# High and low parts of x side by side: one 512-column product in place of two of 256

## The chip, the cores and the metric

One core of one Trainium2 chip. The metric is the device time of one execution in microseconds, median of three runs. Engines: PE multiplies matrices, DVE works on vectors, ACT does activations, copies and casts, POOL is GpSimd, and SP's queue issues most of the DMAs. Granted clock 1.00 is PE at 2.4 GHz, 0.5 is 1.2 GHz.

## What is computed

A decoder trunk for 256 tokens and 2048 channels in float32, with one even and one odd layer (the reference, cut):

```
h = rmsnorm(x, e_norm); z = h @ e_w_in            # 2048 x 6784
a_in, a_gate, q, kB, vB, b_gate = split(z)
yA = rwkv7_mix(a_in, ...)                         # token shift, recurrence over tokens, 16 heads x 64
yB = swa_sinks(rope(q), rope(kB), vB, sinks)      # window 128, 16 query heads, 4 key heads
x = x + concat(yA * silu(a_gate), yB * silu(b_gate)) @ e_w_out
h = rmsnorm(x, o_norm); u, vv, gate = split(h @ o_w_in)      # 2048 x 6144
x = x + (chunked_sgu(u, vv, ...) * silu(gate)) @ o_w_out
return rmsnorm(x, final_norm)
```

## The kernel before

Channels lie on partitions, and x is kept transposed as 16 blocks `k` of 128 channels x 256 tokens. All four weights stream from HBM once, in chunks of 128 x 1024 float32 (512 KB); there are 266 chunks.

**Products in parts.** PE multiplies float32r operands, which round a float32. So each operand is split into a high part (rounded to float32r) and a low part (what the rounding leaves), and a product is high x high + high x low + low x high. `chunk` (L265) loads `raw`, casts it on ACT to `wh`, and on DVE subtracts to get `wl`. These two are traced with priority, so that they stand ahead of other work in ACT's and DVE's queues, and each of the three buffers (`raw`, `wh`, `wl`) exists three times.

**Two kinds of tiles.** A tile of kind B (105 of them: 41 in the even input product, 32 in the odd one, 16 in each output product) gives 128 output channels for 256 tokens. A block of the weight is stationary and x streams: `half_b` (L275) issues three matmuls of 256 columns for each k, 8 k to a chunk, 2 chunks to a tile. The stationary operand is loaded for each matmul, also where two in a row have the same one. A tile of kind A (3 in the even layer for key/value and queries, 4 in the odd one) gives 512 output channels for 2 x 128 tokens: x is stationary, 512 weight columns stream, and `eighth_a` (L301) issues 12 matmuls of 512 columns for a chunk of 2 k. The results of both lie in a PSUM pool of three buffers of 512 columns, of which a B tile uses half.

**Order of the work.** `products` (L312) goes through the tiles. `done(i, ps)` takes a finished tile, and after each chunk `pace` (L257) lets a planner (`Later`, L142) trace further steps of the queued tasks (recurrence, attention, norms) between the chunks, as long as its estimate of DVE's and ACT's time is not ahead of its estimate of PE's. Those estimates come from `Timed`: for PE the columns / 2400 + 0.004 us for a float32r matmul (L135), for DVE elements / 960 + 0.06, for ACT elements / 1200 + 0.1. Engines then work in the order laid down when the program is built.

**What takes a finished tile** (PSUM to SBUF):
- Even layer, `e_done` (L1061): the first B tile carries the low-rank inputs (`scaled`, then `lora_task`, whose tanh lies before the low-rank products `pw`, `pa`); then 8 head pairs with three tiles each (keys, receptance, values), which `shift` (L595) reads from PSUM with one ACT and one DVE pass. Tiles before number X_NEW = 7 go through `scaled` (L589), one DVE pass that multiplies by the norm `rs1`. Then `k_task`, `r_task`, `v_task`: the keys end in `stk` (L688), which the products `m` (L715) need. 16 tiles are gates (`gate`, L1041): ACT's tanh and a DVE pass, both from PSUM. During the first eight gates the triangular solve (`solve_task`, L752) runs on DVE; during the queries and the last eight the recurrence and attention.
- Output product of the even layer, two passes over half of the rows each: `first_done` (L1113) adds a tile to x by one DVE pass, `resid_done` (L1125) adds it, splits the result for the next product (`x1h`, `x1l`) and squares it on POOL.
- Odd layer, `o_done` (L1201): the 32 B tiles are u (one DVE pass, times the norm) and gate, in turn, with `sgu_task` (L1188) behind every second one.
- Last product, `last_done` (L1228): one addition, then squares and scale; then the last norm.

**Around the start.** POOL computes rotary tables (`rope_tables`, L534) in small buffers with the tags of `k1` (L228), and, in between, masks (`setup_task`, L474), among them `blk`, `blkr` and `cen`. `msum` in `rms_rows` (L423) needs the buffer of tag "y", which the rotary table holds up to L570; `tt` of the rotary table holds tag "Pi" up to the end of the second `poly` (L557).

Of the kernel before, what the change touches and what calls it, by code (L numbers as in the profile page):

```python
# [109 lines left out]
class Hold(float):  # L110
    """for how many chunks a queue rests after a step"""


class Timed:
    """An engine with an estimate of how long its work takes, in us."""
# [26 lines left out]
class Later:  # L142
    """Work that is traced in between the chunks of the weight products, as far as the engines keep up."""
# [50 lines left out]
def kernel(ctx, tc, xT, w_in, w_out, o_in, o_out, cols, rows, loras, sinks, pos, ws_t, ws_b, out, dbg=None):  # L194
# [33 lines left out]
    def k1(s, tag, dt=F32):  # L228
        return t1.tile([P, 260], dt, tag=tag, bufs=2 if tag in ("kp", "rp", "vp") else 1, name=nm(s))
# [45 lines left out]
    def half_b(pss, drams, ah, al, half, first, last):  # L275
        for ps, d in zip(pss, drams):
            wh, wl = chunk(d)
            for k in range(8):
                kt = half * 8 + k
                c = slice(k * P, (k + 1) * P)  # L280
                for i, (w, a) in enumerate(((wh, ah), (wh, al), (wl, ah))):
                    TE.matmul(ps[:, 0:T], w[:, c], a(kt), start=(first and k == 0 and i == 0),
                              stop=(last and k == 7 and i == 2))

    def first_chunk(dram):
        """the first of all: in two halves, so that the products start early"""
# [7 lines left out]
        for i in range(2):  # L294
            c = slice(512 * i, 512 * i + 512)
            xh_of(i)
# [4 lines left out]
    def eighth_a(ps, dram, ah, al, q):  # L301
        wh, wl = first_chunk(dram) if not seen else chunk(dram)
        for k in range(2):
            kt = 2 * q + k
            c = slice(k * 512, (k + 1) * 512)
            for h in range(2):
                t = slice(h * P, (h + 1) * P)
                for i, (w, a) in enumerate(((wh, ah), (wh, al), (wl, ah))):
                    TE.matmul(ps[h], a(kt)[:, t], w[:, c], start=(kt == 0 and i == 0),
                              stop=(kt == NK - 1 and i == 2))  # L310

    def products(order, dram, ah, al, done, lead=0, halves=(0, 1)):  # L312
        """One pass over a weight (or over half of its rows); done(i, psum) takes each finished tile.
        The first `lead` tiles go by halves, so that the inputs of the second half may come late."""
# [5 lines left out]
        def tiles(ids):  # L320
            pss = [acc("ps") for _ in ids]
            for n, half in enumerate(halves):
                end = n == len(halves) - 1
                half_b(pss, [dram[base[i] + half] for i in ids], ah, al, half, n == 0, end)
# [7 lines left out]
        for i in range(lead, len(order)):  # L332
            if order[i][0] == "B":
                tiles([i])
            else:
                ps = (acc("psa"), acc("psb"))
                for q in range(8):
                    eighth_a(ps, dram[base[i] + q], ah, al, q)
# [24 lines left out]
    xh, xl = pairs_of(NK, "xh", F32R), pairs_of(NK, "xl", F32R)  # L363
# [5 lines left out]
    def xh_of(k):  # L369
        if state.get("normed"):  # L370
            return xn[k][0]
        if k not in seen:
# [3 lines left out]
            split(xh[k], xl[k], xs[:, k], col(C_GE, k))  # L376
        return xh[k]

    def xl_of(k):
        return xn[k][1] if state.get("normed") else xl[k]  # L380
# [4 lines left out]
    def scale_task():  # L385
        """x times its norm, split anew"""
        for q in range(8):
# [3 lines left out]
            h, l = pairs_of(2, "xnh", F32R), pairs_of(2, "xnl", F32R)  # L391
            for i in range(2):
                xn[2 * q + i] = h[i], l[i]
                split(h[i], l[i], xs[:, 2 * q + i], col(C_GE, 2 * q + i))
# [3 lines left out]
    # the tensor engine's clock is up when the first weights are in  # L398
# [12 lines left out]
    def newton(y, a):  # L411
        """y <- y (1.5 - 0.5 a y^2)"""
# [10 lines left out]
    def rms_rows(parts, rs):  # L423
        """rs[p, t] = (mean of squares over channels + eps)^-1/2 on every partition"""
# [9 lines left out]
    def rms_cols(parts, rc, mc):  # L434
        """the same with tokens on partitions: [P, 2], a column for each half"""
# [36 lines left out]
    sm = {}  # L472

    def setup_task():  # L474
# [6 lines left out]
        # decay weights over what their rounding leaves, and the other way round for the rates  # L481
# [6 lines left out]
        blk = const.tile([P, P], F32, name="blk")  # L488
# [41 lines left out]
    # rotary angles: position * inv_freq reduced by 2 pi, then sine and cosine of a quarter of it  # L530
# [51 lines left out]
    # ================= even layer =================  # L582
# [64 lines left out]
    def k_task(p, kp, st):  # L647
# [11 lines left out]
        # exp of the summed log decays, and of their negative  # L659
# [15 lines left out]
        # minus twice the normed key: the correction of y^-1/2 is (3 - ss y^2) / 2  # L675
# [5 lines left out]
        # minus the scaled keys here, their products with the written ones in the other half: they share  # L681
        # the products with the state and the values
# [69 lines left out]
    def solve_task():  # L752
        """(I - M)^-1 of every head and chunk: 32 x 32 blocks on VectorE, then the corner"""
# [551 lines left out]
```

## Time and profile before

| | |
|---|---|
| median of three runs | 920.48 us (919.36 to 920.57) |
| span of the profiled execution | 916.3 us |
| time of the profiled execution itself | not given beside the span; the median of the runs is 4.2 us above it |
| PE busy | 885.4 us, 7086 matmuls |
| DVE busy | 640.1 us |
| ACT busy | 498.5 us |
| POOL busy | 133.5 us |
| read from HBM | 148.45 MB, mean 164 GB/s |

A busy time is the union of an engine's instructions in the profiled execution. Matmuls are pipelined and the end of each is modelled, so their starts tell more than their durations. PEld are the loads of stationary operands, which overlap with PE. "idle before" is the time for which an engine stood before an instruction, with what ended it. Most instructions carry the line of one helper (L126), so groups are told apart by tiles, written out<-in.

### The profile page before, as it was taken

Reading aid. Unit: us, or ns where it says so; the run is one execution under the profiler, and the core shown is the slowest. Engines: PE = TensorE matmul, PEld = TensorE weight load, DVE = VectorE, ACT = ScalarE, POOL = GpSimd, SP = SyncE. Lnnn points to the kernel's source line nnn. Section 1 sums busy time; section 2 is a strip of 40 time slices with the busy share of each in tenths; the row PEclk is TensorE's granted clock in tenths of the full one; section 3 lists DMA queues with packets and bytes.
Section 4 is the critical chain, followed back from the end, with each engine's and each line's share of the span. In section 5 each row is a group of like instructions: output and inputs, shape, how many; then the busy total and the mean of one; then the engine's idle time right before and its main releaser. Section 6 shows DMA issues by size and latency. Waiting matters only on the chain.

```text
span 916.3 us, 17587 instructions
## 1 busy us (share of the span) xinstructions
PE 885.4 (97%) x7086; PEld 823.3 (90%) x7086; DVE 640.1 (70%) x1004; ACT 498.5 (54%) x823; POOL 133.5 (15%) x215
## 2 busy tenths in 40 slices
PE   7889999999999899999999999999999999999994
PEld 6759899999998677889999988889999999999994
DVE  6766888887899954577767965459766666665554
ACT  7557776676644585777544444447344344344441
POOL 8821100000000201000004840000000000004331
PEclk9968999999999999899999999999999999999997
DMA  8522555545555332234675787665555565565652
GB/s 277 166 89 69 164 162 161 168 154 161 156 148 185 135 93 71 70 100 143 195 224 180 264 262 213 193 193 182 176 178 176 175 182 177 171 182 183 185 164 92
DMA packets 44146, 151.68 MB, mean 166 GB/s; under 512 B 5153, under 2 KB 5537, under 8 KB 43809
## 3 DMA queue, kind: packets, MB, share of 16 engines
q1 hardware_dynamic: 43344, 149.52, 53.0%
q8 instruction: 55, 0.90, 0.4%
q10 hardware_dynamic: 720, 1.05, 0.3%
q14 instruction: 27, 0.21, 0.1%
HBM read 148.45 MB, written 2.10 MB: 164 GB/s over the span
## 4 chain that ended last, share of the span: by engine, by line
PE 81%; DVE 10%; POOL 4%; ACT 2%; issue 2%; DMA 1%; DVEq 0%; ACTq 0%; POOLq 0%
PE ps L126 61%; PE psa L126 6%; PE psb L126 5%; DVE wl L126 4%; PE py L126 2%; DVE dd L126 2%; DVE tmp L126 1%; PE pm L126 1%; ACT sc L126 1%; PE m L126 1%; PE po L126 1%; PE ptp L126 1%; PE pw L126 1%; ACT wh L126 1%; PE pa L126 1%
## 5 line engine op out<-in xcount | busy, mean ns | idle before, releaser
L126 DVE TENSOR_TENSOR wl<-raw,wh 128x1024 fp32r<-128x1024 f32 (+1 forms) x267 | 330.5, 1239 | 169.1 <-ACT wh L126 168.6
L126 ACT CAST wh<-raw 128x1024 fp32r<-128x1024 f32 (+1 forms) x267 | 278.6, 1044 | 310.6 <-PE ps L126 173.1
L126 PE MATMUL ps<-xnh,wh 128*128 128x256 f32 x560 | 161.6, 289 | 0.0
L126 PE MATMUL ps<-xnh,wl 128*128 128x256 f32 x560 | 159.8, 285 | 0.6 <-DVE wl L126 0.6
L126 PE MATMUL ps<-xnl,wh 128*128 128x256 f32 x560 | 159.1, 284 | 0.0
L126 PE MATMUL ps<-x1h,wh 128*128 128x256 f32 x512 | 146.1, 285 | 0.0
L126 PE MATMUL ps<-x1h,wl 128*128 128x256 f32 x512 | 144.9, 283 | 0.0
L126 PE MATMUL ps<-x1l,wh 128*128 128x256 f32 x512 | 144.8, 283 | 0.0
L126 PEld LDWEIGHTS ps<-xnh,wh 128*128 128x128 f32 x560 | 107.1, 191 | 2.0 <-issue 1.0
L126 PEld LDWEIGHTS ps<-xnh,wl 128*128 128x128 f32 x560 | 107.3, 192 | 1.4 <-DVE wl L126 0.8
L126 PEld LDWEIGHTS ps<-xnl,wh 128*128 128x128 f32 x560 | 107.2, 191 | 0.2 <-issue 0.2
L126 PEld LDWEIGHTS ps<-x1l,wh 128*128 128x128 f32 x512 | 98.2, 192 | 0.0
L126 PEld LDWEIGHTS ps<-x1h,wh 128*128 128x128 f32 x512 | 98.2, 192 | 0.0
L126 PEld LDWEIGHTS ps<-x1h,wl 128*128 128x128 f32 x512 | 98.2, 192 | 0.0
L126 PE MATMUL ps<-yk,wh 128*128 128x256 f32 x512 | 92.8, 284 | 0.0
L126 PE MATMUL ps<-yo,wh 128*128 128x256 f32 x512 | 92.3, 283 | 0.0
L126 PEld LDWEIGHTS ps<-yk,wh 128*128 128x128 f32 x512 | 79.8, 192 | 1.1 <-DVE x L126 0.8
L126 PEld LDWEIGHTS ps<-yo,wh 128*128 128x128 f32 x512 | 79.9, 192 | 0.0
L126 PE MATMUL ps<-yo,wl 128*128 128x256 f32 x256 | 72.4, 283 | 0.0
L126 PE MATMUL ps<-yk,wl 128*128 128x256 f32 x256 | 72.4, 283 | 0.0
L126 PEld LDWEIGHTS ps<-yo,wl 128*128 128x128 f32 x256 | 49.1, 192 | 0.0
L126 PEld LDWEIGHTS ps<-yk,wl 128*128 128x128 f32 x256 | 49.1, 192 | 0.0
(327 smaller groups left out, 1503.3 us busy)
## 6 DMA issues: line engine op xcount, KB each, us to landing
raw<-in_w_in SPq DMA_DIRECT2D x105, 512.0 KB, 3.7
raw<-in_o_in SPq DMA_DIRECT2D x96, 512.0 KB, 3.7
raw<-in_w_out SPq DMA_DIRECT2D x32, 512.0 KB, 3.7
raw<-in_o_out SPq DMA_DIRECT2D x32, 512.0 KB, 3.6
x<-in_xT SPq DMA_DIRECT2D x8, 256.0 KB, 4.1
xs<-in_xT SPq DMA_DIRECT2D x7, 256.0 KB, 6.5
wst<-in_ws_t SPq DMA_DIRECT2D x1, 1024.0 KB, 5.8
bsb<-in_ws_b SPq DMA_DIRECT2D x1, 1024.0 KB, 7.8
```

The costliest lines, as they stand in the source:

```text
L126: return f(*args, **kw)
```

## The change

x is no longer kept as one tile of high parts and one of low parts, but as one tile for each k with both, `[128, 2, 256]`. In `half_b` the high weights meet both parts in one matmul of 512 columns, whose result fills the whole PSUM buffer (high x high on the left, high x low on the right); the low weights meet the high part of x in a second matmul of 256 columns, added on the left. So a B tile leaves PSUM as two halves, which have to be added: `whole` copies the right half on ACT and adds the left half on DVE; the output products add both halves to x, one DVE pass each. Kind A keeps its three matmuls and only addresses x in another way.

To make room, small buffers have 256 in place of 260 columns (but for one), `blk` uses the small buffer with the tag "Pi" and is later read as `blkr`, and the tag "z" gets two buffers. Comments are removed.

```diff
     def k1(s, tag, dt=F32):
-        return t1.tile([P, 260], dt, tag=tag, bufs=2 if tag in ("kp", "rp", "vp") else 1, name=nm(s))
+        return t1.tile([P, 260 if tag == "Pp" else T], dt, tag=tag, bufs=2 if tag in ("kp", "rp", "vp", "z") else 1, name=nm(s))
...
-    def half_b(pss, drams, ah, al, half, first, last):
+    def half_b(pss, drams, xp, half, first, last):
         for ps, d in zip(pss, drams):
             wh, wl = chunk(d)
             for k in range(8):
-                kt = half * 8 + k
+                x = xp(half * 8 + k)
                 c = slice(k * P, (k + 1) * P)
-                for i, (w, a) in enumerate(((wh, ah), (wh, al), (wl, ah))):
-                    TE.matmul(ps[:, 0:T], w[:, c], a(kt), start=(first and k == 0 and i == 0),
-                              stop=(last and k == 7 and i == 2))
+                TE.matmul(ps.rearrange("p (s t) -> p s t", s=2), wh[:, c], x, start=(first and k == 0), stop=False)
+                TE.matmul(ps[:, 0:T], wl[:, c], x[:, 0], start=False, stop=(last and k == 7))
...
-                for i, (w, a) in enumerate(((wh, ah), (wh, al), (wl, ah))):
-                    TE.matmul(ps[h], a(kt)[:, t], w[:, c], start=(kt == 0 and i == 0),
+                for i, (w, s) in enumerate(((wh, 0), (wh, 1), (wl, 0))):
+                    TE.matmul(ps[h], xp(kt)[:, s, t], w[:, c], start=(kt == 0 and i == 0),
                               stop=(kt == NK - 1 and i == 2))
...
-    xh, xl = pairs_of(NK, "xh", F32R), pairs_of(NK, "xl", F32R)
+    def parts_of(n, s):
+        return [k2(s, F32R).rearrange("p (s t) -> p s t", s=2) for _ in range(n)]
+
+    xp = parts_of(NK, "xp")
...
-            h, l = pairs_of(2, "xnh", F32R), pairs_of(2, "xnl", F32R)
-            for i in range(2):
-                xn[2 * q + i] = h[i], l[i]
-                split(h[i], l[i], xs[:, 2 * q + i], col(C_GE, 2 * q + i))
+            for k, x in zip((2 * q, 2 * q + 1), parts_of(2, "xn")):
+                xn[k] = x
+                split(x[:, 0], x[:, 1], xs[:, k], col(C_GE, k))
                 yield
...
-        blk = const.tile([P, P], F32, name="blk")
+        blk = k1("blk", "Pi")[:, 0:P]
         G.memset(blk, 0.0)
         G.memset(blk[0:64, 0:64], 1.0)
         G.memset(blk[64:128, 64:128], 1.0)
         blkr = const.tile([P, P], F32R, name="blkr")
         G.tensor_copy(blkr, blk)
+        blk = blkr.bitcast(F32)
         cen = const.tile([P, P], F32, name="cen")
...
-    def scaled(ps):
-        z = k1("z", "z")[:, 0:T]
-        V.tensor_tensor(z, ps[:, 0:T], rs1, op=ALU.mult)
+    def whole(ps, z):
+        S.copy(z, ps[:, T:2 * T])
+        V.tensor_tensor(z, z, ps[:, 0:T], op=ALU.add)
         return z
 
+    def scaled(z):
+        V.tensor_tensor(z, z, rs1, op=ALU.mult)
+        return z
...
     def gate(ps, rs, dst, final=False):
         th = k1("th", "kp")[:, 0:T]
-        z = ps[:, 0:T]
+        z = whole(ps, dst)
         if rs is not None:
-            V.tensor_tensor(dst, z, rs, op=ALU.mult)
-            z = dst
+            V.tensor_tensor(z, z, rs, op=ALU.mult)
...
-            later.add("r", lora_task(scaled(ps)))
+            later.add("r", lora_task(scaled(whole(ps, k1("z", "z")[:, 0:T]))))
...
-            z = shift(ps if i >= X_NEW else scaled(ps), E_ORDER[i][1] // P, ("kp", "rp", "vp")[w])
+            z = whole(ps, k1("z", "z")[:, 0:T])
+            z = shift(z if i >= X_NEW else scaled(z), E_ORDER[i][1] // P, ("kp", "rp", "vp")[w])
...
     def first_done(i, ps):
-        V.tensor_tensor(x1[i], x1[i], ps[:, 0:T], op=ALU.add)
+        for s in range(2):
+            V.tensor_tensor(x1[i], x1[i], ps[:, s * T:(s + 1) * T], op=ALU.add)
...
     def resid_done(i, ps):
-        V.tensor_tensor(x1[i], x1[i], ps[:, 0:T], op=ALU.add)
-        split(x1h[i], x1l[i], x1[i], col(C_GO, i))
+        for s in range(2):
+            V.tensor_tensor(x1[i], x1[i], ps[:, s * T:(s + 1) * T], op=ALU.add)
+        split(x1p[i][:, 0], x1p[i][:, 1], x1[i], col(C_GO, i))
...
-            V.tensor_tensor(u, ps[:, 0:T], rs2, op=ALU.mult)
+            V.tensor_tensor(u, whole(ps, u), rs2, op=ALU.mult)
...
     def last_done(i, ps):
-        V.tensor_tensor(x1[i], ps[:, 0:T], x1[i], op=ALU.add)
+        for s in range(2):
+            V.tensor_tensor(x1[i], ps[:, s * T:(s + 1) * T], x1[i], op=ALU.add)
```

## Rows read from the trace of the kernel before

**Rows 1.** The page's parts 1 and 4: busy time of engines, chain that ended last.

```profile
PE 885.4 (97%) x7086; PEld 823.3 (90%) x7086; DVE 640.1 (70%) x1004; ACT 498.5 (54%) x823; POOL 133.5 (15%) x215
...
PE 81%; DVE 10%; POOL 4%; ACT 2%; issue 2%; DMA 1%; DVEq 0%; ACTq 0%; POOLq 0%
```

**Rows 2.** Stretches, instructions on `ps` alone: us from:to, length, busy by engine (count).

```profile
95.68:240.00 144.32, 131.96 (x1065) 128.61 (x1065) 10.33 (x22) 9.62 (x21) 1.00 0.54 162
...
355.00:435.00 80.00, 51.33 (x384) 48.22 (x383) 2.90 (x7) 2.83 (x8) 0.96 0.35 102
435.00:531.00 96.00, 93.36 (x768) 92.42 (x768) 13.28 (x32) 0.17 (x1) 1.00 0.68 220
...
619.00:811.00 192.00, 188.28 (x1538) 185.57 (x1539) 13.53 (x32) 0.00 (x0) 1.00 0.58 177
811.00:903.20 92.20, 92.16 (x768) 91.95 (x767) 6.41 (x17) 0.00 (x0) 1.00 0.53 160
```

**Rows 3.** The chain that ended last, in order of time: start us, us, what.

```profile
198.81 1.09 PE m L126 x16
...
811.00 92.17 PE ps L126 x768
```

**Rows 4.** Stretches: length, busy PE, PEld, DVE, ACT, POOL (count), PEclk, DMA share, GB/s.

```profile
56.00:79.96 23.96, 23.96 (x82) 17.23 (x83) 10.29 (x20) 12.81 (x26) 0.00 (x0) 0.56 0.13 42
79.96:99.73 19.77, 17.85 (x152) 17.39 (x151) 18.45 (x37) 13.38 (x28) 6.06 (x12) 1.00 0.41 133
...
198.58:218.35 19.77, 19.77 (x173) 19.51 (x172) 16.11 (x32) 13.60 (x26) 0.67 (x2) 1.00 0.52 162
240.00:301.00 61.00, 58.56 (x398) 53.03 (x396) 58.54 (x106) 27.60 (x40) 1.47 (x4) 1.00 0.53 162
...
400.00:420.00 20.00, 20.00 (x168) 17.80 (x166) 19.85 (x53) 15.48 (x44) 0.00 (x0) 1.00 0.48 137
435.00:482.00 47.00, 47.00 (x387) 45.11 (x384) 31.14 (x49) 23.14 (x42) 0.00 (x0) 1.00 0.67 208
503.28:511.92 8.64, 8.64 (x75) 8.64 (x74) 7.83 (x9) 4.48 (x7) 6.83 (x7) 1.00 0.60 192
619.00:811.00 192.00, 192.00 (x1605) 191.89 (x1604) 132.22 (x202) 85.53 (x110) 0.00 (x0) 1.00 0.58 177
```

**Rows 5.** Timeline of PE, a tile of kind A: start us, us, engine, instruction.

```profile
532.04 0.39 PE L126 MATMUL psb<-wl,x1h 128*128 128x512 f32 x1
...
533.40 0.39 PE L126 MATMUL psb<-wl,x1h 128*128 128x512 f32 x1
```

**Rows 6.** Timeline of PE at the low granted clock; nine matmuls lie between.

```profile
74.49 0.41 PE L126 MATMUL ps<-xl,wh 128*128 128x256 f32 x1
...
76.63 0.41 PE L126 MATMUL ps<-xh,wl 128*128 128x256 f32 x1
```

**Rows 7.** Groups of instructions by shape, DVE and ACT: busy us, mean ns, idle before.

```profile
L126 DVE TENSOR_TENSOR x<-x,ps 128x256 f32<-128x256 f32 x32 | 13.3, 415 | 11.0 <-PE ps L126 10.5 <-DMA x<-in_xT 0.5
...
L126 DVE SCALAR_TENSOR_TENSOR zp<-ps,colt,zp 128x255 f32<-128x255 f32 x19 | 9.1, 478 | 0.2
...
L126 ACT COPY qT<-pt 128x256 f32<-128x256 f32 x8 | 2.6, 382 | 0.0
```

**Rows 8.** Timeline of DVE in a settled head pair.

```profile
195.42 0.41 DVE L126 SCALAR_TENSOR_TENSOR stk<-y,aPi 64x256 f32<-64x256 f32 x1
195.75 0.41 DVE L126 TENSOR_TENSOR stk<-zp,Pi 64x256 f32<-64x256 f32 x1
...
196.53 0.42 DVE L126 TENSOR_TENSOR stk<-zp,Pi 64x256 f32<-64x256 f32 x1
...
197.38 1.22 DVE L126 TENSOR_TENSOR wl<-raw,wh 128x1024 fp32r<-128x1024 f32 x1
```

**Rows 9.** Timeline of POOL near the start.

```profile
5.50 0.76 POOL L493 CAST blkr<-blk 128x128 fp32r<-128x128 f32 x1
```

**Rows 10.** Timeline of DVE before the first norm, with the idle time before.

```profile
38.30 0.42 DVE L126 TENSOR_SCALAR msum<-rms 128x256 f32<-128x256 f32 x1 [3.08 <-POOL rt L570]
```

More of the change, by code (lines that the diff above doesn't have):

```diff
@@ L110 @@
 class Hold(float):
+    pass
 class Timed:
@@ L295, in first_chunk @@
             c = slice(512 * i, 512 * i + 512)
-            xh_of(i)
+            x_of(i)
             S.copy(wh[:, c], raw[:, c])
@@ L299, in first_chunk, with eighth_a @@
         return wh, wl
-    def eighth_a(ps, dram, ah, al, q):
+    def eighth_a(ps, dram, xp, q):
         wh, wl = first_chunk(dram) if not seen else chunk(dram)
@@ L307, in eighth_a, with products @@
                 t = slice(h * P, (h + 1) * P)
-                for i, (w, a) in enumerate(((wh, ah), (wh, al), (wl, ah))):
-                    TE.matmul(ps[h], a(kt)[:, t], w[:, c], start=(kt == 0 and i == 0),
+                for i, (w, s) in enumerate(((wh, 0), (wh, 1), (wl, 0))):
+                    TE.matmul(ps[h], xp(kt)[:, s, t], w[:, c], start=(kt == 0 and i == 0),
                               stop=(kt == NK - 1 and i == 2))
-    def products(order, dram, ah, al, done, lead=0, halves=(0, 1)):
+    def products(order, dram, xp, done, lead=0, halves=(0, 1)):
         base, at = [], 0
@@ L323, in tiles @@
                 end = n == len(halves) - 1
-                half_b(pss, [dram[base[i] + half] for i in ids], ah, al, half, n == 0, end)
+                half_b(pss, [dram[base[i] + half] for i in ids], xp, half, n == 0, end)
                 for i, ps in zip(ids, pss):
@@ L337, in products @@
                 for q in range(8):
-                    eighth_a(ps, dram[base[i] + q], ah, al, q)
+                    eighth_a(ps, dram[base[i] + q], xp, q)
                     if q == 7:
@@ L367, in split, with x_of @@
         V.scalar_tensor_tensor(dst_l, src, g, dst_h.bitcast(F32), op0=ALU.mult, op1=ALU.subtract)
-    def xh_of(k):
+    def x_of(k):
         if state.get("normed"):
-            return xn[k][0]
+            return xn[k]
         if k not in seen:
@@ L375, in xh_of @@
                 load_x(q)
[L376 to L380, printed above, removed]
+            split(xp[k][:, 0], xp[k][:, 1], xs[:, k], col(C_GE, k))
+        return xp[k]
     seen = set()
@@ L1107 @@
     later.add("a", setup_task())
-    products(E_ORDER, w_in, xh_of, xl_of, e_done)
+    products(E_ORDER, w_in, x_of, e_done)
     x1t = [k2("x1").rearrange("p (a t) -> p a t", a=2) for _ in range(8)]
@@ L1120 @@
     later.finish("n")
-    products(M_ORDER, w_out, lambda k: yk[k][:, 0], lambda k: yk[k][:, 1], first_done, halves=(0,), lead=LEAD1)
+    products(M_ORDER, w_out, lambda k: yk[k], first_done, halves=(0,), lead=LEAD1)
     later.finish()
-    x1h, x1l = pairs_of(NK, "x1h", F32R), pairs_of(NK, "x1l", F32R)
+    x1p = parts_of(NK, "x1p")
     def resid_done(i, ps):
-        V.tensor_tensor(x1[i], x1[i], ps[:, 0:T], op=ALU.add)
-        split(x1h[i], x1l[i], x1[i], col(C_GO, i))
+        for s in range(2):
+            V.tensor_tensor(x1[i], x1[i], ps[:, s * T:(s + 1) * T], op=ALU.add)
+        split(x1p[i][:, 0], x1p[i][:, 1], x1[i], col(C_GO, i))
         if i == 0:
@@ L1133, in resid_done @@
             G.tensor_tensor(ssa, ssa, sq, op=ALU.add)
-    products(M_ORDER, w_out, lambda k: yk[k][:, 0], lambda k: yk[k][:, 1], resid_done, halves=(1,), lead=LEAD2)
+    products(M_ORDER, w_out, lambda k: yk[k], resid_done, halves=(1,), lead=LEAD2)
     rs2 = rs1
@@ L1222 @@
     state["slack"] = SLACK3
-    products(O_ORDER, o_in, lambda k: x1h[k], lambda k: x1l[k], o_done)
+    products(O_ORDER, o_in, lambda k: x1p[k], o_done)
     last = {}
     def last_done(i, ps):
-        V.tensor_tensor(x1[i], ps[:, 0:T], x1[i], op=ALU.add)
+        for s in range(2):
+            V.tensor_tensor(x1[i], ps[:, s * T:(s + 1) * T], x1[i], op=ALU.add)
         if i == 0:
@@ L1239, in last_done @@
         S.activation(x1[i], x1[i], AF.Copy, scale=col(C_GF, i))
-    products(M_ORDER, o_out, lambda k: yo[k][:, 0], lambda k: yo[k][:, 1], last_done, lead=LEAD4)
+    products(M_ORDER, o_out, lambda k: yo[k], last_done, lead=LEAD4)
     rms_rows([ssa, last["sq"]], rs2)
```

## The prediction

> **What bounds the kernel now.** I read the shares of the page first, then the chain that ended last, then the span by stretches. PE is busy 97% of the span and holds 81% of the chain; DVE holds 10% [rows 1]. A PE whose ends are modelled may look busy while it waits, so the question is where its matmuls follow each other without a gap. The 128x256 products into `ps`, which the change rewrites, are counted by stretch in [rows 2]: 1065 from 95.68 to 240 us (the head pairs), 384 from 355 to 435 (the last gates, beside recurrence and attention), 768 in the first output product, 1538 in the odd layer's narrow tiles, 768 in the last product. In the last one the chain is a single piece, 768 matmuls in 92.17 us [rows 3], 120.0 ns each, which is bound by PE and nothing else.
>
> DVE is second. By stretch [rows 4]: from 240 to 301 us (the solve) it is busy 58.54 of 61.00 us and sets the pace itself; from 79.96 to 99.73 it has 18.45 of 19.77; in a settled head pair 16.11 of 19.77; from 400 to 420 19.85 of 20.00; in three chunks of the second output pass 7.83 of 8.64; in the odd layer's narrow tiles 132.22 of 192.00. A saving on PE is paid in full only where DVE can take more work.
>
> **What a matmul less is worth.** The tiles of kind A are 512 columns wide already. Six of them start from 532.04 to 533.40 us [rows 5]: 1.36 / 6 = 0.2267 us. What a column costs is seen where the granted clock is low: from 74.49 to 76.63 us ten matmuls of 256 columns take 2.14 us [rows 6], 214 ns each, a column a cycle at 1.2 GHz. At 2.4 GHz (granted clock 1.00 in the stretches above) 512 columns are then 213.3 ns and 256 are 106.7, and both widths pay the same 13.3 ns beyond their columns: 226.7 = 213.3 + 13.3, 120.0 = 106.7 + 13.3. Per k the kernel now pays 3 x 120.0 = 360.0 ns, and will pay 226.7 + 120.0 = 346.7. A chunk (8 k) falls from 2.88 to 2.77 us. No row shows a 512 next to a 256, so the bounds are 333.3 ns (768 columns in 320 ns and one remainder) and 360.0 (no gain). I take 346.7, since two independent widths give the same remainder.
>
> A rule speaks against this size. The Trainium skill, "TensorE: Matmul & The Clock Gate", section "Wait — 56ns, not 53.3ns?", puts the fixed part of a warm matmul at about 2.5 ns. The trace disagrees with it: 13.3 at both widths. By the page the sum would gain 1380 x 2.5 ns = 3.5 us on PE (the 1380 k of the next paragraph), less than the added passes cost.
>
> Where PE is the bound: 1065 + 768 + 1538 + 768 = 4139 matmuls are 1380 k, x 13.3 ns = 18.4 us. From 355 to 435 us 128 k are worth 1.7; PE shares that stretch with serial work, so I take half, 0.9. Nothing is counted from 240 to 301 (DVE sets the end) nor from 56 to 79.96, where the mean granted clock is 0.56 [rows 4] and 256 columns show no remainder to save. **Gain 19.3 us**, at most 20.1.
>
> **What the change adds.** `whole` runs 73 times (25 tiles of the pairs and low ranks, 16 even gates, 32 odd tiles): an ACT copy of 256 columns from PSUM, 382 ns by the nearest row, and a DVE addition with a PSUM operand, 415 ns [rows 7]. The three passes of the output products add 48 more additions of 415 ns. That is 27.9 us of ACT and 121 x 0.415 = 50.2 us of DVE. The later passes that then read SBUF instead of PSUM keep their price: the shift's takes 478 ns from `ps` [rows 7], more than the addition, so that the place of its operand is not what sets it. ACT was busy 54% [rows 1], so I cost its copies only where they lengthen a chain. DVE's additions, by stretch:
> - *Solve, 240 to 301.* DVE is full. Of the first eight gates, which the code sets beside the solve, I count seven here, and in a full queue a pass of this size moves the next by 0.33 us (195.42 to 195.75 in [rows 8]). 7 x 0.33 = **+2.3** (to 2.9 at the full 0.415).
> - *79.96 to 99.73 and the low ranks.* The six tiles before x is normed add 2.5 us about here, to a DVE with 1.3 us free; I take half, 1.2. The low-rank tile's copy and addition, 0.8 us, stand straight in the way of the tanh that its products wait for. **+2.0** (0 to 3.3).
> - *Settled pairs.* 16.11 + 3 x 0.415 = 17.36 against a new period of 19.77 - 48 x 0.0133 = 19.13: it fits. The copy and addition delay a pair's keys by 0.8 us, two more additions ahead of them in the queue by 0.8, and PE comes 0.4 earlier: 2.0 in all. Now the last `stk` ends at 196.95 and the products `m` start at 198.81 [rows 8, 3], a slack of 1.86. So at most some tenths a pair: **+0.5** (0 to 3).
> - *400 to 420.* DVE is full; of the last eight gates, spread from 355 to 435, two or three fall here: up to 1.2, of which PE work hides part. **+0.7** (0 to 2).
> - *First output pass.* DVE has 31.14 of 47.00 [rows 4]; 16 x 0.415 = 6.6 fits: 0.
> - *Second output pass.* Three chunks need 7.83 + 1.25 = 9.08 us of DVE against 8.32 of PE: 0.25 us of lag a chunk, 4.0 over 16. The evictions fall behind, not the splits, which are traced with priority; three PSUM buffers let PE run two chunks (5.5 us) ahead, and the 512-wide tiles behind leave DVE room to catch up. **+1.0** (0 to 4.0).
> - *Odd layer and last product.* 132.22 + 32 x 0.415 = 145.5 of 185: 0.
> - *End.* The last tile's second addition follows the first on the chain: **+0.4**.
>
> **The rest.** `blk` moves into the buffer of tag Pi, so its POOL work (the cast of 0.76 us [rows 9] and five smaller passes, about 2.2 us) has to wait for the rotary table to leave it, on the queue that the norm waits for (3.08 us before `msum` [rows 10]). The same passes leave the front of that queue and come back behind, most likely before the pass that releases `msum`: 0, between -2.2 and +1. Two buffers for z remove waits, and I price that at nothing. No DMA is moved or added, and SP's queue keeps its order. The planner's PE estimate per k falls from 0.332 to 0.328 us, by its own formula, while its DVE and ACT estimates rise by some 0.3 us a tile: later steps come a little later, and the pairs' queue has emptied by then in any case.
>
> **Sum.** -19.3 + 2.3 + 2.0 + 0.5 + 0.7 + 1.0 + 0.4 = -12.4 us. The profiled span of 916.3 becomes 903.9. The profiled execution's own time is not given beside its span; the median of the runs is 4.2 us above it, and I carry that over: 920.48 - 12.4 = **908** us.
>
> **Rivals.**
> - *DVE's waits stay shut (slower).* DVE works in order, and its idle time in a pair (3.66 us) or in three chunks of the second pass (0.81) may be waits for ACT's `wh` that no addition can fill. Then a pair takes 19.77 + 1.25 = 21.02 instead of 19.13, x 7.3 pairs = 13.8, and a chunk of the second pass 2.88 + 0.415 instead of 2.77, x 16 = 8.3. In place of my 1.5 for the two that gives 908 + 20.6 = 929. It makes the kernel slower than before from the point at which six tenths of these waits stay shut. For it: splits have priority and DVE queues behind them. Against it: in [rows 8] passes already run back to back up to the next split at 197.38. Chance 0.06.
> - *The remainder goes with the columns, not with the instruction (slower).* If reading 512 columns of x costs two remainders, a k stays at 360.0 and all of the gain is gone: 908 + 19.3 = 927. [Rows 5] speak against it: there x is the stationary side, though, and the weights stream. Chance 0.04. The skill's 2.5 ns, named above, ends near here: 908 + 19.3 - 3.5 = 924; since the trace has 13.3 it gets 0.02.
> - *Part of both.* A third to a half of the waits stay shut: 917 to 922. Chance 0.08.
> - *All additions are hidden* but the solve's and the end's, and POOL's chain gets shorter: 920.48 - 20.1 + 2.7 - 2.2 = 901; with a cheaper pair than 346.7 below 900. Chance of under 900: 0.04.
> - That the products are not what the diff says (split into two of 256) has nothing for it: 512 columns run as one instruction today [rows 5].
>
> **How the numbers follow.** The forecast with its unknown costs at their bounds runs from 901 to 920.48 - 19.3 + 15.6 (all upper ends) + 1 = 918, and holds 0.76. A range of 900 to 917 leaves out the 0.04 below, the 0.12 of the slower rivals and most of the middle case, about 0.2. A measurement of this kernel tells 0.2% (1.8 us) from no change. Faster than 918.6: 0.76 + 0.04 + 0.05 of the middle case = 0.85; within 0.2%: 0.03; slower: 0.12.
>
> **What would show it.** Right: about 1680 matmuls fewer, the last product as 512 matmuls in about 88.8 us, head pairs of 19.1 to 19.5 us, the solve's stretch 2 to 3 us longer, DVE at about 690 us of busy time, the second output pass with DVE busy to the full. Wrong: a k of the last product at 360 ns; pairs of 20 us or more with PE idle behind DVE's additions; PE waiting for an accumulator at the second output pass; or a start that shifts by more than 3 us, which I have not priced.

## The result and the profile after

The changed kernel takes 932.59 us (median of four runs, 932.09 to 938.52) beside 920.53 of the kernel before: ratio 1.015, interval 1.012 to 1.018. It is slower by 12 us where 12 were to be gained, and outside the predicted range. The profiled execution took 932.51 us with a span of 930.3, 14.0 longer than the span before.

The page of the changed kernel, its parts 1 and 4 (busy times, and the chain by engine), answers to [rows 1]:

```profile
PE 892.4 (96%) x5406; PEld 746.5 (80%) x5406; DVE 677.3 (73%) x1125; ACT 519.7 (56%) x898; POOL 136.9 (15%) x215
...
PE 79%; DVE 11%; POOL 3%; ACT 2%; issue 2%; DMA 2%; DVEq 0%; ACTq 0%; POOLq 0%
```

The 1680 matmuls are gone and 121 DVE instructions have come, as foreseen. Yet PE is busy for longer than before, with fewer matmuls. In part that is its clock, granted at 0.965 on average beside 0.974; in part it is how busy time is read, since a stretch of serial matmuls that wait for each other also shows as busy (from 400 to 420 us below, 20.00 of 20.00 us with 108 matmuls, where [rows 4] has 168). The end of the chain (start us, us, what) is as predicted, beside [rows 3]:

```profile
827.88 88.77 PE ps L126 x512
916.67 0.44 DVE x L126
917.13 0.43 DVE x L126
```

512 matmuls in 88.77 us, and one more addition of 0.43 at the end. So the loss lies earlier. Stretches of the changed kernel (columns as in [rows 4]):

```profile
240.00:301.00 61.00, 60.54 (x326) 51.25 (x326) 59.52 (x112) 33.39 (x53) 2.68 (x6) 1.00 0.48 172
301.00:321.00 20.00, 11.59 (x153) 9.49 (x152) 19.63 (x25) 5.29 (x9) 0.90 (x3) 0.79 0.21 71
400.00:420.00 20.00, 20.00 (x108) 15.04 (x106) 5.75 (x9) 10.93 (x19) 0.00 (x0) 0.79 0.15 54
500.00:508.64 8.64, 8.64 (x51) 7.51 (x50) 7.00 (x11) 3.76 (x5) 0.61 (x1) 1.00 0.51 181
641.52:827.60 186.08, 186.08 (x1088) 163.31 (x1087) 140.91 (x231) 92.82 (x141) 0.00 (x0) 1.00 0.52 181
```

From 400 to 420 us DVE had 19.85 us of work before [rows 4]; now it has 5.75, ACT 10.93, and the granted clock is 0.79. That is the shape of serial work which nothing fills, at a time when before it was over. PE's largest wait between 240 and 510 us, from the waits of PE:

```profile
PE px L126 <- DVE sc L126: 7.4, 1, 7.4
```

And the chain there:

```profile
312.80 1.89 DVE et L126
314.72 1.89 DVE et L126
316.65 0.44 DVE sc L126
317.13 4.82 PE px L126 x126
```

`px`, the first products behind the solve, stand next in PE's order while DVE still transposes `et` and begins on `sc`, and PE runs nothing in between. When they run, 126 of them take 4.82 us. In the kernel before all 128 take less than half of that (timeline of PE):

```profile
309.52 2.21 PE L126 MATMUL px<-et,Tm 32*32 32x32 f32 x128
```

The mean granted clock from 301 to 321 us is 0.79, so a part of the stretch is at the lower of the two levels. The Trainium skill, "TensorE: Matmul & The Clock Gate", section "HAM oscillation — how this bites in real kernels", says that an engine left waiting loses its clock and starts the next group slow. The trace agrees: PE stood 7.4 us just before.

The second loss is in the odd layer's tiles of kind A, 94.4 us from their first matmul to the first B tile, 88.6 before. The chain there:

```profile
551.44 4.87 DMA raw<-in_o_in
556.40 1.06 ACT wh L126
557.48 0.95 DVE wl L126
558.43 7.68 DMA raw<-in_o_in
566.21 1.05 ACT wh L126
```

A weight chunk that arrives late, on a queue whose order the prediction had called unchanged. PE stands 3.7 us for its `wh` and 0.5 for its `wl`, and from 570 to 574 us the granted clock is 0.73: the matmuls behind the wait run slowly, which makes up the rest of the 5.8 us.

### The profile page after: what moved, and what is told of

It reads as the page before. It is cut to its first block, busy times and chain, and to the rows that moved or that the text cites. A ratio compares the mean times of both kernels' runs of the same rounds, so it can differ in the third digit from the quotient of the medians.

```text
span 930.3 us, 14423 instructions
## 1 busy us (share of the span) xinstructions
PE 892.4 (96%) x5406; PEld 746.5 (80%) x5406; DVE 677.3 (73%) x1125; ACT 519.7 (56%) x898; POOL 136.9 (15%) x215
## 4 chain that ended last, share of the span: by engine, by line
PE 79%; DVE 11%; POOL 3%; ACT 2%; issue 2%; DMA 2%; DVEq 0%; ACTq 0%; POOLq 0%
PE ps L126 58%; PE psa L126 5%; PE psb L126 5%; DVE wl L126 4%; PE py L126 2%; DMA raw<-in_o_in 1%; DVE dd L126 1%; DVE et L126 1%; PE m L126 1%; DVE tmp L126 1%; PE po L126 1%; PE psc L126 1%; ACT wh L126 1%; PE pm L126 1%; PE px L126 1%
## 5 line engine op out<-in xcount | busy, mean ns | idle before, releaser
L126 PE MATMUL ps<-xn,wh 128*128 128x512 f32 x560 | 204.1, 405 | 1.5 <-DVE z L126 0.7
L126 PE MATMUL ps<-x1p,wh 128*128 128x512 f32 x512 | 181.0, 397 | 0.0
L126 PE MATMUL ps<-xn,wl 128*128 128x256 f32 x560 | 160.7, 288 | 0.5 <-DVE wl L126 0.5
L126 PE MATMUL ps<-x1p,wl 128*128 128x256 f32 x512 | 143.2, 280 | 0.0
L126 PEld LDWEIGHTS ps<-xn,wh 128*128 128x128 f32 x560 | 106.9, 191 | 26.9 <-issue 1.4
L126 PEld LDWEIGHTS ps<-x1p,wh 128*128 128x128 f32 x512 | 96.1, 188 | 22.0
L126 PEld LDWEIGHTS ps<-xn,wl 128*128 128x128 f32 x560 | 107.7, 192 | 3.2 <-DVE wl L126 1.1
L126 PEld LDWEIGHTS ps<-x1p,wl 128*128 128x128 f32 x512 | 96.6, 189 | 0.0
L126 PE MATMUL ps<-yk,wh 128*128 128x512 f32 x256 | 91.2, 400 | 0.3 <-DVE yk L126 0.3
L126 PE MATMUL ps<-yo,wh 128*128 128x512 f32 x256 | 88.9, 391 | 0.0
```

The source lines that it names most:

```text
L126: return f(*args, **kw)
```

## The experiments

In the kernels below `wide(stage, i)` says whether tile i of a stage is multiplied wide; a narrow tile goes by three matmuls of 256 columns and leaves PSUM by the passes of the kernel before. Stages are e (even input product), f and r (the two output passes), o (odd input product), l (last product). The theories: **A**, the added passes fill DVE and ACT and make the work late; **B**, the smaller edits cost; **C**, the wide product saves little; **P**, the planner. P was formed only after six runs.

The table collects all of them: the weight chunks that PE has multiplied ahead of the first `px` (counted from the trace by the `wl` matmuls, 8 a chunk in a B tile, 4 in an A tile), starts in us of the first `px` and of the first output product, the length of the odd kind A tiles, and the median. The medians are of different rounds, in which the kernel before took 919.3 to 920.5 us; each ratio further on is to the kernel before of the same round.

| kernel | chunks ahead of px | px | output product | odd A tiles | median |
|---|---|---|---|---|---|
| before | 84 | 309.5 | 435.5 | 88.6 | 920.5 |
| changed | 85 | 309.5 (then stands 7.4) | 447.3 | 94.4 | 932.6 |
| x1 no passes | 84 | 302.3 | 430.5 | 96.0 | 911.6 |
| x2 passes only | 85 | 315.5 | 437.0 | 95.0 | 931.1 |
| x3 odd and last wide | 84 | 307.8 | 433.8 | 94.4 | 913.9 |
| x4 first gates narrow | 84 | 307.7 | 438.8 | 95.6 | 918.5 |
| x5 smaller edits only | 84 | 306.9 | 435.1 | 93.9 | 923.8 |
| x6 first gates only wide | 85 | 316.0 | 450.4 | 93.6 | 940.5 |
| x7 even narrow, loads spread | 84 | 306.6 | 434.7 | 89.4 | 909.8 |
| x8 the same, in twos | 84 | 307.2 | 432.0 | 90.7 | 906.1 |
| x9 planner told only | 85 | 313.2 | 442.4 | 94.4 | 932.4 |
| x10 first gates wide, not counted | 84 | 302.1 | 438.0 | 93.8 | 925.8 |
| x11 change, not counted | 84 | 304.0 | 437.9 | 96.1 | 916.4 |
| x12 x11 and loads spread | 84 | 305.6 | 438.9 | 89.5 | 911.6 |
| x13 x8 and pairs from tile 7 | 84 | 309.7 | 435.7 | 90.0 | 908.1 |

**x1: the wide product without its passes.**

```diff
     def whole(ps, z=None):
-        S.copy(z, ps[:, T:2 * T])
-        V.tensor_tensor(z, z, ps[:, 0:T], op=ALU.add)
-        return z
+        return ps[:, 0:T]
...
-        for s in range(2):
+        for s in range(1):
             V.tensor_tensor(x1[i], x1[i], ps[:, s * T:(s + 1) * T], op=ALU.add)
```

> The wide products stay; a finished narrow-kind tile is taken from its left half alone, by the passes of the kernel before, so the product of the high weights with the low part of x is left out of those tiles. If the added passes on DVE and ACT are what costs (theory A), only the saving on PE is left: 1380 k at 6.7 to 13.3 ns, 9 to 18 us below 920.5, that is 902 to 911 us. If the smaller edits (blk in another buffer, buffers of 256 columns, x in pairs, two z) are what costs (rival B), it stays at 920 us or above. If the wide product is worth little by itself (rival C), 915 to 920 us.

911.64 us, ratio 0.991 (0.989 to 0.993). The kind A tiles lose 7.4 us here too, without any added pass, so the rest gains 7.7 + 7.4 = 15.1 us. C falls; A and B both keep a part.

**x2: the passes without the wide product.**

```diff
-                TE.matmul(ps.rearrange("p (s t) -> p s t", s=2), wh[:, c], x, start=(first and k == 0), stop=False)
-                TE.matmul(ps[:, 0:T], wl[:, c], x[:, 0], start=False, stop=(last and k == 7))
+                for i, (m, s) in enumerate(((wh, 0), (wh, 1), (wl, 0))):
+                    TE.matmul(ps[:, (i == 1) * T:(i == 1) * T + T], m[:, c], x[:, s], start=False,
+                              stop=(last and k == 7 and i == 2))
```

> The passes of the changed kernel stay (ACT copy and DVE addition of the right half, two additions in the output products), but PE goes back to three matmuls of 256 columns for each k: high x high and low x high to the left half, high x low to the right; only the first k of a tile keeps the wide matmul. Nothing of the result is left out. Theory A: the passes alone cost what the change lost plus what PE had saved: 932.6 + 9 to 14 = 941 to 947 us, with PE standing before the products of the recurrence as in the changed kernel. If the passes were hidden and the wide product were what hurts (rival C), about 921 us.

931.11 us, ratio 1.013 (1.011 to 1.014), 10 less than theory A asked for. The passes alone cost 11.8 us, of which 6.4 in the kind A tiles. But the two parts do not add: -7.7 and +11.8 make +4.1, the change has +12.1. (Both hold the smaller edits as well; with these counted once, at the 4.2 us of x5 below, the parts make -0.1.) Something else depends on both.

**x3: wide in the odd layer and the last product alone.**

```diff
 def wide(stage, i):
-    return True
+    return stage in "ol"
```

> Wide only in the odd layer's input product and in the last product; the even layer and its output product go by three matmuls of 256 columns and leave PSUM as before. Theory A: the odd layer and the last product have DVE to spare, so 920.5 - 5.4 (odd) - 3.4 (last) + 0.5 (end) = 912 us, and the odd tiles of kind A do not wait for their weights. If the smaller edits cost (B), 918 us or above, since they are all still in.

913.91 us, ratio 0.994 (0.992 to 0.996), and PE does stand 4.3 us in the kind A tiles. The even layer has the products and passes of the kernel before here, and its output product starts 1.7 us earlier, so the stall does not come from a late attention.

**x4: the first eight gates narrow.**

```diff
 def wide(stage, i):
-    return True
+    return not (stage == "e" and 26 <= i < 34)
```

> The changed kernel with the first eight gates of the even layer (those beside the solve) by three matmuls of 256 columns and leaving PSUM as before. Theory A: eight copies and additions go out of the stretch in which DVE is full, PE no longer stands for 7.6 us before the first product of the recurrence and its clock stays up: 932.6 - 7 to - 10 = 922.5 to 925.5 us. If the solve is late for another reason, or the time lost there is lost elsewhere (rival D: the layout of the queues shifted, any edit moves it), 930 to 934 us.

918.48 us, ratio 0.998 (0.997 to 1.000): 14.1 us come back by eight tiles (12.9 with each beside the kernel before of its round), more than the 7 to 10 that A gave, though 128 k lose the wide product. PE no longer stands at `px`. The place was right, but eight additions of 0.408 us, 3.3 us in all, can hardly be what costs that much.

**x5: the smaller edits alone.**

```diff
 def wide(stage, i):
-    return True
+    return False
```

> Three matmuls of 256 columns everywhere and tiles leave PSUM as in the kernel before; only the smaller edits stay (blk in the buffer of tag Pi, small buffers of 256 columns, x in one tile for each k, two z). The runs so far all show 94 to 96 us for the odd layer's tiles of kind A, with PE standing 4 to 6 us for a weight chunk, also where the even layer is as before. Theory B2 (the smaller edits put the eight loads of lnw and lnb two chunks later in SP's queue): the start gains 1.7 us as in the run with only the odd layer wide, the kind A tiles take 94 to 95 us instead of 88.6, in all 923 to 926 us. If the stall belongs to the wide product or its passes (theory A2): 918 to 920 us and 88.6 us for these tiles.

923.80 us, ratio 1.004 (1.003 to 1.006); 93.9 us for the kind A tiles: B2 holds. The order of SP's queue shows why. Timeline of SP, kernel before:

```profile
518.94 6.57 SPq L267 DMA_DIRECT2D raw<-in_o_in  x3
525.56 0.42 SPq L251 DMA_DIRECT2D lnw<-in_rows  x1
...
530.84 31.44 SPq L267 DMA_DIRECT2D raw<-in_o_in  x13
```

The same of x5:

```profile
518.49 14.69 SPq L275 DMA_DIRECT2D raw<-in_o_in  x5
533.24 0.42 SPq L259 DMA_DIRECT2D lnw<-in_rows  x1
...
539.50 21.31 SPq L275 DMA_DIRECT2D raw<-in_o_in  x9
```

And of the changed kernel:

```profile
535.42 16.34 SPq L267 DMA_DIRECT2D raw<-in_o_in  x6
551.86 0.39 SPq L251 DMA_DIRECT2D lnw<-in_rows  x1
...
558.43 3.03 SPq L267 DMA_DIRECT2D raw<-in_o_in  x3
```

The eight loads (2 MB) stood behind three weight chunks of the odd layer, now behind five or six. Before, the block of loads fell while PE was still in the output product (up to 530.88 us) and had three chunks in hand, and the next chunk came just in time; now it falls inside the kind A tiles, and that chunk comes too late. Which of the smaller edits moves these loads in the built order, and why, was not tested.

**x6: the first eight gates alone wide.**

```diff
 def wide(stage, i):
-    return True
+    return stage == "e" and 26 <= i < 34
```

> The counterpart of the run with narrow gates: wide product and added passes in the first eight gates of the even layer alone, all else by three matmuls of 256 columns. Theory A: the eight gates by themselves make the solve late; on top of the smaller edits' 3 to 5 us they cost 10 to 14 us, 932 to 939 us, with PE standing before px or the recurrence late by 8 us or more. Theory A3 (they cost only together with the pairs, whose later work the solve inherits): 925 to 929 us.

940.47 us, ratio 1.023 (1.021 to 1.025), more than either theory: 16.7 us over x5. DVE ends the solve (its last `et`) only 3.4 us later than in x5, 313.5 against 310.1. So some 13 us are not explained by DVE's later end. What x2, x6 and the changed kernel share is the second column of the table: 85 chunks ahead of `px` in place of 84, and with it the recurrence and the attention move back by one to two chunks (in x6 the recurrence's first `pR` runs behind 87 chunks, in x5 behind 86; the attention's last `po` behind 115 and 113). In which chunk a step is traced is decided by the planner, from estimates in which every added pass counts. That is theory P.

**x7: even input product narrow, loads spread.**

```diff
 def wide(stage, i):
-    return True
+    return stage != "e"
...
-    for b in range(4):
+    def load_ln(b):
         c = slice(512 * b, 512 * b + 512)
         load_here(lnw[b], rows[0:1, c].to_broadcast([P, 512]))
         load_here(lnb[b], rows[1:2, c].to_broadcast([P, 512]))
...
                 V.bn_stats(bst[:, h, i], vln[:, h, 512 * i:512 * i + 512])
+            if i < 2:
+                load_ln(2 * i)
+                load_ln(2 * i + 1)
```

> Wide in both output products and in the odd layer, narrow in the whole input product of the even layer; and the eight loads of lnw and lnb (2 MB) no longer stand in one block in SP's queue, but four behind the first tile of kind A of the odd layer and four behind the second. If the block of loads is what PE waits for in the kind A tiles (B2), these tiles go from 94.4 us back to 88.6 to 90, and with 1.5 us from the output product the kernel takes 913.9 - 5 - 1.5 = 907 us (905 to 909). If the wait has another cause, 912 us or more.

909.80 us, ratio 0.989 (0.987 to 0.991), just above the expected 905 to 909; the kind A tiles are back at 89.4 us, and PE waits there for no load.

**x8: the same, matmuls in twos.**

```diff
-                TE.matmul(ps[:, 0:T], wl[:, c], x[:, 0], start=False, stop=(last and k == 7))
+                for j in range(k - 1, k + 1) if k % 2 else ():
+                    TE.matmul(ps[:, 0:T], wl[:, j * P:(j + 1) * P], xp(half * 8 + j)[:, 0], start=False, stop=(last and j == 7))
```

> As the run with the spread loads, and the wide tiles issue their matmuls in twos: high weights of k and k+1 (512, 512), then low weights of both (256, 256). The traces show two beats of the 512 and 256 in turn, 346.7 ns for a k or 353.3 (three k in 1060 ns), by stretch. If the beat comes from the alternation of widths, 1536 k at the slower one gain up to 6.7 ns each where they had it: in the odd B tiles (351.5 ns on average) some 2.5 us, in the output product 1 us: 903 to 905 us. If the beat is of another cause, no change within 1.5 us; if a change of width costs by itself, 2 us or more to gain in the last product too, which has 346.7 now.

906.09 us, ratio 0.986 (0.984 to 0.987): the fastest of all kernels here, 14 us below the one before, but above the expected 903 to 905. By the starts of their first and last matmuls the odd B tiles gain 0.5 us over x7, the output product 1.3, the last product loses 0.4 and the kind A tiles 1.3; 2.1 come between the last `py` and the output product, where the order of the queues differs a little. The order of the widths does change the beat, only not to the better of the two: where matmuls follow each other without other work, a k takes 348.4 to 348.8 ns on average in all three places, while x7 has 353.4 in the output product, 350.4 in the odd B tiles (both beats mixed) and 346.8 in the last product. So one place gains and another loses. (The wide tiles have 1024 k here, not 1536.)

**x9: the planner told, nothing done.** All tiles narrow as in x5, and:

```diff
+                        if stage == "e" and 26 <= i < 34:
+                            S.t += T / 1200 + 0.1
+                            V.t += T / 960 + 0.06
                         done(i, ps)
```

> As the run with the smaller edits alone (923.8 us; no wide product, no added pass), but for each of the first eight gates the planner's estimates are raised by what it would count for an ACT copy (0.313 us) and a DVE addition (0.327 us) of 256 columns. Nothing more is executed. Theory P (the planner, which counts the added passes, lays the steps of solve, recurrence and attention later among the weight chunks, so that the recurrence meets fewer chunks and PE's clock falls): most of the 16.7 us of the eight wide gates come without any added work, 932 us or more. Theory A (the passes themselves fill DVE and make the solve late): 922 to 926 us.

932.40 us, ratio 1.012 (1.008 to 1.016): 8.6 us lost to x5 without one instruction more. Stretches of x5:

```profile
300.00:320.00 20.00, 17.60 (x315) 13.65 (x315) 19.48 (x26) 9.97 (x26) 3.83 (x4) 0.91 0.42 134
320.00:340.00 20.00, 19.28 (x222) 15.20 (x218) 9.32 (x14) 16.41 (x31) 0.00 (x0) 1.00 0.30 90
```

and of x9:

```profile
300.00:320.00 20.00, 18.71 (x220) 14.73 (x221) 17.85 (x25) 7.20 (x23) 3.80 (x4) 0.91 0.43 134
320.00:340.00 20.00, 18.61 (x206) 14.44 (x203) 6.53 (x8) 13.87 (x26) 0.00 (x0) 0.66 0.21 61
```

`px` comes at 313.2 instead of 306.9 us. From 320 to 340 DVE and ACT have less to do, and the clock is 0.66 instead of 1.00: the chain of recurrence runs later, and more of it at half clock.

**x10: the first eight gates wide, not counted.** As x6, but the passes run past the planner's books, and a wide k counts like three narrow matmuls:

```diff
     def whole(ps, z=None):
-        S.copy(z, ps[:, T:2 * T])
-        V.tensor_tensor(z, z, ps[:, 0:T], op=ALU.add)
+        nc.scalar.copy(z, ps[:, T:2 * T])
+        nc.vector.tensor_tensor(z, z, ps[:, 0:T], op=ALU.add)
         return z
...
                 if w:
+                    TE.t += 0.004
```

> As the run with the first eight gates alone wide (940.5 us): the same products and passes are executed, but the planner does not count the eight copies and additions and counts the wide product as three matmuls of 256 columns. Theory P: the order is that of the narrow kernel again, what is left is the 2.3 to 3.4 us by which the solve ends later: 924 to 929 us. Theory A: 936 us or more.

925.84 us, ratio 1.007 (1.004 to 1.009): P. The clock tells the same; x6, then x10, from 360 us on:

```profile
360.00:380.00 20.00, 20.00 (x174) 15.11 (x174) 4.10 (x8) 9.12 (x16) 0.00 (x0) 0.76 0.15 54
400.00:420.00 20.00, 20.00 (x125) 16.51 (x125) 6.15 (x8) 10.87 (x19) 0.00 (x0) 0.74 0.22 61
```

```profile
360.00:380.00 20.00, 20.00 (x273) 16.77 (x273) 11.21 (x20) 14.45 (x30) 2.15 (x6) 1.00 0.26 81
400.00:420.00 20.00, 20.00 (x168) 18.43 (x167) 19.86 (x48) 15.50 (x41) 0.00 (x0) 1.00 0.38 114
```

The four kernels that differ in the first eight gates alone make a square (medians):

| | not counted | counted |
|---|---|---|
| narrow, no added pass | 923.8 (x5) | 932.4 (x9) |
| wide, with the passes | 925.8 (x10) | 940.5 (x6) |

The work costs 2.0 us, net of whatever the wide product saves in these tiles; the count costs 8.6 without the work and 14.7 with it. The two counts are not quite the same: in x6 the planner also takes the wide product for 0.5 us shorter (128 k at 0.004 us), in x9 it does not. Nor can the clock be all of it. From 300 to 440 us, by the mean granted clock of the stretches 300 to 340 and 340 to 440, x9 is granted 6.8 us less of full clock than x5, and x6 7.8 less than x10; by this estimate that is the most that the clock can cost there.

**x11: the whole change, not counted.** All tiles wide, `whole` as in x10, the second additions of the output and last products uncounted likewise.

> The changed kernel whole, all its products and passes, but the planner counts none of the added copies and additions, and a k as before. Theory P: the solve and the recurrence go back to within 4 us of the kernel before; the stall of the kind A tiles (5 to 6 us) and the savings of the odd layer stay: 915 to 922 us. Theory A: 929 to 934 us.

916.38 us, ratio 0.997 (0.996 to 0.998): 16.2 us of the change's time are the planner's count (15.0 with each beside the kernel before of its round). From 400 to 420 us DVE has its work again, and the clock is full:

```profile
400.00:420.00 20.00, 20.00 (x123) 16.05 (x122) 18.48 (x42) 15.01 (x38) 0.00 (x0) 1.00 0.34 116
```

The recurrence's last `py` starts at 389.8 us; in the changed kernel it starts at 405.7, in the one before at 388.0. So 15.9 of the 16.2 us lie ahead of that point. The kind A tiles still take 96.1 us.

**x12: x11 with the loads spread** (the edits of x11 and x7).

> The changed kernel whole, with the added passes not counted by the planner (916.4 us) and the eight loads of lnw and lnb spread behind the first two tiles of kind A in the odd layer. If the two causes found, the planner's order and the block of loads, account for the miss, the kind A tiles go from 96.1 us to 89.5 and the kernel takes 909 to 912 us, inside the predicted range. If something else of the change costs as much (the passes themselves on DVE, theory A), 914 us or more.

911.63 us, ratio 0.991 (0.989 to 0.993), inside the predicted range; kind A tiles 89.5 us. With all products and passes of the change executed, two repairs to the order take 21 us off it. That leaves a gain of 8.8 us beside the kernel before of its round, where the prediction's sum had 12.4.

**x13: pairs wide from tile 7** (as x8, `stage != "e" or 7 <= i < 26`, nothing counted).

> As the run with the matmuls in twos (906.1 us: wide in both output products and the odd layer, loads spread), and also wide in the head pairs from tile 7 on, where x is already normed; the planner counts none of the added passes. With the order unchanged the pairs take 19.45 instead of 19.78 us (so the run not counted showed), 6 pairs = 2.0 us: 904 us. If the pairs' shorter time only makes the solve wait for DVE or the order after it move: 906 us or more.

908.11 us, ratio 0.987 (0.986 to 0.989), 2.0 over x8 (1.2 with each beside the kernel before of its round, and the two intervals overlap): the gain of 2.0 did not come. x13 also leaves uncounted the added passes of the later products, which x8 counts, so the two differ by more than the pairs. A pair takes 20.0 us, not 19.45. That figure was a mean of five pairs in x11, one of 18.01 us and four of 19.71 to 20.05; a settled pair was never at 19.45 with the passes. The chain at a settled pair of x13, beside the 1.09 us of [rows 3]:

```profile
198.12 1.86 PE m L134 x16
```

and DVE ahead of it:

```profile
195.30 0.41 DVE L611 TENSOR_TENSOR z<-z,ps 128x256 f32<-128x256 f32 x1
...
196.36 1.21 DVE L134 TENSOR_TENSOR wl<-raw,wh 128x1024 fp32r<-128x1024 f32 x1
197.50 0.41 DVE L134 TENSOR_TENSOR stk<-zp,Pi 64x256 f32<-64x256 f32 x1
...
198.28 0.42 DVE L134 TENSOR_TENSOR stk<-zp,Pi 64x256 f32<-64x256 f32 x1
```

The addition and a `wl` stand ahead of `stk`. Its second half is written at 198.70, when `m` has begun on the first.

## Why the prediction was wrong, point by point

- **The planner (the step that failed).** The prediction saw the estimates change ("later steps come a little later, and the pairs' queue has emptied by then in any case") and costed it at nothing. It looked at the pairs and not at the next queue, the solve and recurrence, which are long, serial and share the planner with the first gates. The count moved them by one weight chunk. With nothing executed, the count of the first eight gates alone costs 8.6 us (x9 over x5); leaving all added passes uncounted gives 16.2 back (932.6 - 916.4).
- **SP's queue.** "No DMA is moved or added, and SP's queue keeps its order" was wrong for the eight loads of `lnw` and `lnb`. Alone (x5) the smaller edits cost 4.2 us, 5.3 lost in the kind A tiles against a start that gains 1.1; undone by spreading, 4.8 (x11 to x12; 6.7 in the kind A tiles themselves).
- **PE's gain.** 19.3 us were predicted; without passes and without the stall x1 gains 15.1, of which some 1.1 are the smaller edits' at the start. The price of 346.7 ns a k, estimated without a row of the two widths side by side, is right in the last product (88.77 us) and too good elsewhere: there many k take 353.3 (below). The odd B tiles gain 5.2 us, not 6.8.
- **The solve, +2.3.** About right: 2.0 (x10 over x5), and DVE ends the solve 1.9 us later there. What x4 and x6 showed beyond that was not DVE's work.
- **The start, +2.0.** From the start to the second pair's `m` the change loses 2.6 us and the smaller edits alone gain 1.1, so the passes cost some 3.7, above the upper end of 3.3.
- **Head pairs.** 19.13 us and some tenths were predicted, against 19.77 before. x1, without the passes, has 19.50. With them a settled pair gains nothing: the change has 19.94 on average, and x12, in good order, 19.70 to 20.05 in four pairs and 18.02 in one (19.49 on average). So these 355 k, worth 4.7 us in the sum, gave little, and the +0.5 was too small. The slack of 1.86 us between `stk` and `m` was read from the last `stk`; x13 shows that it counts as well how far apart the halves of `stk` come.
- **DVE's busy time** rose by 37.2, not 50.2 us: 121 passes at 0.31 on average, since busy time counts overlapping passes once ([rows 8] had 0.33 from start to start), not at the 0.41 that one lasts alone. The prediction had used this for the solve and not for the whole.
- **Second output pass, +1.0; last product; end, +0.4.** Right: the second pass gains 0.9 us (45.2 from 46.1) where its 128 k alone are worth 1.7, so 0.8 are given back; the last product gains 3.4; the end loses 0.43. The first output pass, costed at nothing, takes 54.5 us instead of 49.3, but 48.5 in x11: with the late order the attention's matmuls run inside it (the last `po` starts 34.4 us behind its start, 23.0 before).
- **The rivals.** "DVE's waits stay shut" gave 929 and comes near the time, but not by its mechanism: the second output pass takes less time than before, with DVE at 7.00 of 8.64 us, and x12 executes all the same passes in 911.6. No rival named the order of the work, which the prediction had dismissed in half a sentence.

Open remains how the shift by one chunk makes its price. At the start of the second output pass the four kernels with 85 chunks are later than x5 by 6.6 us (x2), 9.2 (x9), 17.2 (x6) and 17.5 (the change), so the same shift has no single price, and that counting costs 8.6 us without the passes and 14.7 with them is not explained. Open is also what chooses between the two beats of the widths.

## What to carry to other kernels

A kernel whose order is laid by a planner with its own estimates has two prices for an added pass: what it takes on the engine, and what its estimate moves. Separate them by two cheap kernels, one that is told and does nothing, one that does and is not told. Before a price of nothing is written for "the order is kept", follow each long serial chain and each block of loads to the first place where it could slip by one step, and ask what PE would then be without.

## What the runs showed of the hardware

The pair of 512 and 256 columns has two beats. PE's timeline in the last product of the changed kernel, five k with three of them left out:

```profile
849.91 0.39 PE L126 MATMUL ps<-yo,wh 128*128 128x512 f32 x1
...
851.29 0.39 PE L126 MATMUL ps<-yo,wh 128*128 128x512 f32 x1
```

The same instructions of the same product in x1:

```profile
849.79 0.40 PE L134 MATMUL ps<-yo,wh 128*128 128x512 f32 x1
...
851.20 0.40 PE L134 MATMUL ps<-yo,wh 128*128 128x512 f32 x1
```

From the first line to the last are four k: 1.38 us against 1.41. To the nanosecond the starts follow each other by 230 and 117 in turn in the first, and by 236, 241 and 233 with 113 to 120 between in the second, three k in 1060: 346.7 and 353.3 a k. The last product keeps its beat from start to end in each kernel; in the odd B tiles both occur. Both kernels issue the same matmuls there, and in twos (x8) there is a third beat, 348 to 349 a k.

The `m` matmuls use 64 rows each. In the kernel before their raw starts come in twos, 6 ns apart, one of each half, every 112 ns; where the second half's `stk` is late (x13), the first eight come singly, most of them 112 ns apart, and the block takes 1.86 us for 1.09. So the pairing is lost with it. Whether the late operand breaks it or the built order, which may differ in x13, is not shown.
